# Which PSUM banks a decoder's token mixers take: single banks for columns and projections, pairs for spatial products, scores and turns

## The chip, the cores and the metric

The kernel runs on one core of a Trainium2 chip. The metric is the device time of one execution in microseconds (us). Times of single instructions come from a profile of one execution; they are counted from the start of its span.

## The reference

Two decoder layers over 256 positions of width 1024, in float32. Layer 0 mixes positions with a chunked gMLP (mixer A), layer 1 with block-sparse attention that at this length is plain causal attention over one block with a relative-position bias (mixer B, MoBA). After each mixer comes a gated MLP with a causal convolution of width 3, and after each of the four parts x <- LayerNorm(alpha x + f(x)).

```python
def chunked_gmlp(x, w_in, ln_g, ln_b, w_s, b_s, w_out):
    z = jax.nn.gelu(x @ w_in)
    u, v = jnp.split(z, 2, axis=-1)
    v = layer_norm(v, ln_g, ln_b)
    v = v.reshape(B, nc, GMLP_CHUNK, GMLP_GROUPS, GMLP_GROUP_DIM)
    w = jnp.where(causal[None], w_s, jnp.zeros_like(w_s))
    sv = jnp.einsum('gts,bnsgc->bntgc', w, v) + b_s.T[None, None, :, :, None]
    return (u * sv.reshape(B, S, GMLP_WIDTH)) @ w_out

def moba_attention(x, w_qkv, w_o, rel_bias):   # cut to what is left at S = 256
    q, k, v = ...                               # 16 heads of 64, q scaled
    s = q @ k.T + bias[rel_bucket(t - s)]       # -inf above the diagonal
    return softmax(s) @ v @ w_o

def conv_ffn(x, w_up, conv_w, conv_b, w_down):
    h = x @ w_up
    hc = conv_b + sum(conv_w[j] * shifted(h, j) for j in range(3))
    g, val = jnp.split(hc, 2, axis=-1)
    return (jax.nn.gelu(g) * val) @ w_down
```

## The kernel before

Every large product is made of float32 operands split in two parts, a high one (rounded by ScalarE, a Copy) and a low one (what is left, a subtraction on VectorE); three products high x high, high x low, low x high are added up in PSUM. Weights come by DMA in chunks of 1 MB into two buffers (raw) and are split into whi and wlo, of which ten half chunks are kept; the next chunk's loading is written down when the last product of an earlier one is (`spent`).

The program first writes down every operation in a plan, each with its engine, its cost and the buffers that it reads and writes. The planner (`Plan.emit`) then plays the plan through with these costs and gives each engine's instructions an order. On TensorE the bulk products keep the order in which they were written down; operations marked fill (spatial products, scores, turns, applies, transposes) go between them, as soon as the plan believes their inputs ready. Each engine then runs its order strictly, and waits where an input is late. `plan.later(ns, fn)` writes something down only after so many ns of TensorE's planned work.

PSUM has eight banks of 512 columns. Four are tiles of their own (`bank0` to `bank3` in the program, drawn as `bank`), four are the halves of two tiles of two banks each (`twos0`, `twos1`, the pairs; drawn as `twos`). The choice of a bank is made when an operation is written down:

```python
    def bank(long=False):
        free = [i for i in ALONE if not bank_of[i][2]]
        return taken(min(free, key=lambda i: bank_of[i][0]), long) if free else half(long)

    def couple(j):
        return j + BANKS // 2, j + BANKS // 2 + len(twos)

    def half(long=False):

        j = min((j for j in range(len(twos)) if not all(bank_of[i][2] for i in couple(j))),
                key=lambda j: max(bank_of[i][0] for i in couple(j)))
        return taken(min((i for i in couple(j) if not bank_of[i][2]), key=lambda i: bank_of[i][0]), long)
```

So `bank()` gives the single bank that was taken longest ago (a half, if all four are held for long), `half()` a half of the pair that was taken longest ago, `couple(j)` names the two halves of pair j, and `taken(i, long)` takes bank i and lets its new user wait for the one before. The plan follows banks; the program that is made from it guards tiles by its own means.

- Mixer A (`gmlp`): the v half of the input product goes by rows into the four single banks, held for long, until a GELU on ScalarE reads them; then v is normalized on VectorE. The u half goes by columns of 128: eight columns g, each of 24 products of 256 columns (`cols_times`) into a `half()`, and a GELU on ScalarE. The spatial product of group g (`spatial`, fill) also goes into a `half()`; VectorE adds the bias and multiplies by u. Five of them are written down between the columns, three during the output product (`project_out("a_out")`), whose four row pieces are single banks.
- MoBA (`moba`): the values go by rows into the halves of the two pairs (row block t = 0 into pair 0, t = 1 into pair 1), products over k = 0 to 4 for both row blocks first, then the rest, then the split. At that time the last two pieces of the down-projection before it (`project_out("f_dn0")`) and the transposes of its LayerNorm are still being read. For each pair of heads i then: q and k as columns (`project(i, 0)` and `project(i, 1)`, 24 products each into a `half()`, then a copy, a high and a low part), scores of the pair before (`scores`, two single banks, one for each head), the softmax on VectorE and ScalarE, turns (`turn`: three transposes of each head into a single bank, then the split), applies (`apply`, one bank). The last turns and applies are written down during the output product (`project_out("b_o")`), whose four row pieces are the four single banks.
- The up-projection (`conv_up`) uses both pairs in turn, two banks at a time.

In the rows below a line of the program can be that of a helper: L326 is a product (`mms`), L332 a transpose, L338 a ScalarE operation (`act`), L344 a VectorE operation of two tensors (`tt`), L348 one with a scalar, L351 the normalization, L825 to L834 the softmax. Tile names: xt is the transposed x, `ff` and `rr` are two large scratch buffers (q, k, u, softmax; h, v, applied heads), `qk` the parts of q and k.

Of the kernel before, what the change touches and what calls it, by code (L numbers as in the profile page):

```python
# [18 lines left out]
P = 128  # L19
# [6 lines left out]
NT = S // P  # L26
# [197 lines left out]
def trunk_kernel(ctx: ExitStack, tc: tile.TileContext, a: dict, out: bass.AP):  # L224
# [53 lines left out]
    def taken(i, long):  # L278
        old = bank_of[i][1]
        b = Buf(banks[i], [old] if old else [])  # L280
        state["age"] += 1
        bank_of[i] = (state["age"], b, long)
        return b
# [13 lines that stand above are left out]
# [342 lines left out]
    def gmlp():  # L639
        at = xt_at(xh, xl)  # L640
        pieces = [[(o, HALF, bank(True)) for o in (0, HALF)] for _ in range(NT)]
        order = [(k, t) for k in range(4) for t in range(NT)] + [(k, t) for t in range(NT) for k in range(4, KT)]
        v = []
        for k, t in order:
            rows_step(pieces[t], *at(k, t), *sub("a_v", k // 2, k % 2), k == 0, k == KT - 1)
            if t == NT - 1 and k % 2:
                spent("a_v", k // 2)
            if (k, t) == (3, NT - 1):
                rows = ln_rows(0)
                ws, bs = load_mixer()  # L650
            if k == KT - 1:
                vt = place("ff", HALF + t * D, D)
                for o, n, b in pieces[t]:
                    act(vt.ap[:, o:o + n], b.ap, AF.Gelu_apprx_tanh, [b], [(vt, range(o // S, (o + n) // S))],
                        psum=True, table="gelu")
                    done_with(b)
                st, mean, rstd = stats(vt, vt.ap, [(0, HALF), (HALF, HALF)])
                scaled(vt, vt.ap, st, mean, rstd, rows)
                v.append(vt)
        load_rest()  # L660
        mh, ml = place("rr", 0, KT * S), place("rr", KT * S, KT * S)
        hv, lv = (b.ap.rearrange("p (k s) -> p k s", k=KT) for b in (mh, ml))
        uring = Places("ff", [0, S, HALF + 2 * D, HALF + 2 * D + S], S)
        yring = Places("ff", range(5120, 6144, S), S)
        us = {}

        def spatial(g):
            b, y = half(), yring.new()
            mms([(b.ap[:, c * P:(c + 1) * P], v[c].ap[:, g * P:(g + 1) * P], ws[1][:, g, :], True, True)
                 for c in range(NT)], [(v[c], [g // 2]) for c in range(NT)] + [ws[0]], [b], fill=True)  # L670
            y3 = y.ap.rearrange("p (c t) -> p c t", c=NT)
            tt(y3, b.ap[:, :S].rearrange("p (c t) -> p c t", c=NT), bs[1][:, g:g + 1, :].to_broadcast([P, NT, P]),
               ALU.add, [b, bs[0]], [y])
            tt(y.ap, y.ap, us[g].ap, ALU.mult, [y, us[g]], [y])
            split((mh, [g], hv[:, g, :]), (ml, [g], lv[:, g, :]), (y, [0], y.ap))

        for g in range(GROUPS):
            b = half()
            cols_times(b, xh, xl, *sub("a_u", g // 2, g % 2))
            if g % 2:  # L680
                spent("a_u", g // 2)
            us[g] = uring.new()
            act(us[g].ap, b.ap[:, :S], AF.Gelu_apprx_tanh, [b], [us[g]], psum=True, table="gelu")
            if g >= 3:
                spatial(g - 3)
        for g in range(GROUPS - 3, GROUPS):
            plan.later(600 * (g - GROUPS + 4), lambda g=g: spatial(g))
        return lambda k, t: (hv[:, k, t * P:(t + 1) * P], lv[:, k, t * P:(t + 1) * P], [(mh, [k]), (ml, [k])])
# [69 lines left out]
    def moba(h, l, scr):  # L758
# [9 lines left out]
        ohv, olv = (b.ap.rearrange("p (k s) -> p k s", k=KT) for b in (oh, ol))  # L768
        vhv, vlv = (b.ap.rearrange("p (t d) -> p t d", t=NT) for b in (vh, vl))
        at = xt_at(h, l)  # L770
        pieces = [[(o, HALF, taken(i, True)) for o, i in zip((0, HALF), couple(j))] for j in range(NT)]
        for ks in (range(5), range(5, KT)):
            for t in range(NT):
                for k in ks:
# [10 lines left out]
        held, biases = {}, {}  # L785

        def project(i, j):
            b, t = half(), qkring[j].new()
            cols_times(b, h, l, *sub("b_qk", i, j))

            n, at2, scale = (P, P, DH ** -0.5) if j == 0 else (S, 0, 1.0)
            src, (th, tl) = b.ap[:, at2:at2 + n], (x.new() for x in qkparts[j])
            act(t.ap, b.ap[:, :P], AF.Copy, [b], [t], scale=scale, psum=True)
            act(th.ap, src, AF.Copy, [b], [th], scale=scale, psum=True)
            stt(tl.ap, src, scale, th.ap.bitcast(F32), ALU.mult, ALU.subtract, [b, th], [tl])
            t = (t, th, tl)
            held.setdefault(i, []).append(t)
            if j == 0:
                biases[i] = bring.new()
                load(biases[i].ap, bass.AP(tensor=scr.ap.tensor, offset=scr.ap.offset + 2 * i * DIST,  # L800
                                           ap=[[1, P], [DIST, 2], [1, S]]), [biases[i]], [scr])
            else:
                spent("b_qk", i)

        def scores(i):
            ((q0, qh, ql), (k0, kh, kl)), bias = held[i], biases[i]
            bank2 = [bank() for _ in range(2)]


            def both(o, seq):  # L810
                return [(bank2[hh].ap[:, o[0]:o[1]], x.ap[hh * DH:(hh + 1) * DH], y.ap[hh * DH:(hh + 1) * DH],
                         n == 0, n == len(seq) - 1) for n, (x, y) in enumerate(seq) for hh in range(2)]

            mms(both((0, P), [(q0, k0)]) + both((P, P + S), [(qh, kh), (qh, kl), (ql, kh)]),
                [q0, qh, ql, k0, kh, kl], bank2, fill=True)
            held[i] = [softmax(bank2[hh], bias, hh) for hh in range(2)]
# [20 lines left out]

        def turn(i):
            ph, pl = (x.new() for x in pring)
            for hh in range(2):  # L840
                e, b = held[i][hh], bank()

                transposes([(b.ap[:, c * P:(c + 1) * P], e.ap[:, c * P:(c + 1) * P]) for c in range(3)],
                           [(e, [0, 1])], [b])
                sl = slice(hh * (P + S), (hh + 1) * (P + S))
                split((ph, [hh], ph.ap[:, sl]), (pl, [hh], pl.ap[:, sl]), (b, [0], b.ap[:, :P + S]), psum=True)
            held[i] = ph, pl
# [124 lines left out]
```

## Time and profile before

| what | value |
|---|---|
| time, median of 3 runs | 578.51 us (577.9 to 579.87) |
| profiled execution: its own time | 579.16 us |
| profiled execution: span from first to last instruction | 577.5 us |
| mean granted TensorE clock, share of full speed | 0.997 |
| TensorE (PE) busy | 560.1 us, 97% of the span |
| VectorE (DVE) busy | 473.7 us, 82% |
| ScalarE (ACT) busy | 361.9 us, 63% |

A busy time is the sum over an engine's instructions, where they overlap counted once. The ends of products are modelled: 0.28 us for a product of 256 columns, though the next one starts earlier. A row of the order of time gives start, duration, engine, line, operation, output <- inputs, shapes and how many were merged; in brackets stands how long the engine was idle before it, and what ended that.

### The profile page before, as it was taken

The page shows a single profiled execution, that of the slowest core. Times are in us where ns is not written, and L with a number is a line of the kernel's source. Part 1 is how long each engine was busy: PE and PEld are TensorE (multiplying, and loading weights), DVE is VectorE, ACT ScalarE, POOL GpSimd, SP SyncE. Part 2 cuts the span into 40 slices and gives each one's busy share as a digit, 9 for nine tenths or more (in the row PEclk, how much of TensorE's full clock was granted, in tenths as well). Part 3 has the DMA queues.
Part 4 walks back from the last instruction along what each step waited for, and adds up shares of the span by engine and source line. Part 5 has one row for each costly group of instructions (what it writes and reads, how often), then busy time and mean ns, then how long its engine had stood idle before and what let it go on. Part 6 is the DMA issues. An engine that isn't in the chain of part 4 may idle for free.

```text
span 577.5 us, 8559 instructions
## 1 busy us (share of the span) xinstructions
PE 560.1 (97%) x3210; PEld 485.9 (84%) x3210; DVE 473.7 (82%) x885; ACT 361.9 (63%) x660; POOL 11.3 (2%) x17
## 2 busy tenths in 40 slices
PE   6998999999999999999999999999999999999994
PEld 4798888888888878888889998888888888888884
DVE  5587989999999997558878889879999999996426
ACT  5555567776677685435568777658777778785300
POOL 0020010000000000001000000000000000000001
PEclk9999999999999999999999999999999999999998
DMA  7887544537454567742663442515456555567202
GB/s 260 330 336 274 199 145 151 215 145 259 188 211 156 210 230 267 259 169 87 250 250 117 181 165 92 201 73 183 183 188 254 199 170 211 219 218 255 110 1 73
DMA packets 20133, 110.93 MB, mean 192 GB/s; under 512 B 2251, under 2 KB 6268, under 8 KB 7676
## 3 DMA queue, kind: packets, MB, share of 16 engines
q1 hardware_dynamic: 20092, 110.39, 53.0%
q8 instruction: 25, 0.41, 0.3%
q14 instruction: 16, 0.13, 0.1%
HBM read 109.31 MB, written 1.07 MB: 191 GB/s over the span
## 4 chain that ended last, share of the span: by engine, by line
PE 92%; DVE 3%; DMA 2%; ACT 2%; issue 0%; SPq 0%; DVEq 0%; ACTq 0%
PE twos L326 60%; PE bank L326 29%; DMA raw<-in_a_v 2%; PE bank L332 2%; DVE wlo L344 1%; DVE rr L344 1%; ACT ff L338 1%; DVE x L348 0%; ACT whi L338 0%; ACT rr L338 0%; SPq L355 0%; DVE ff L825 0%; PE twos L332 0%; DVE ff L834 0%; DVE stat L494 0%
## 5 line engine op out<-in xcount | busy, mean ns | idle before, releaser
L326 PE MATMUL twos<-xt,whi 128*128 128x512 f32 (+1 forms) x1024 | 295.1, 354 | 2.0 <-ACT ff L338 1.5
L344 DVE TENSOR_TENSOR wlo<-raw,whi 128x1024 fp32r<-128x1024 f32 (+1 forms) x212 | 228.4, 1098 | 30.8 <-ACT whi L338 30.3
L326 PE MATMUL twos<-xt,wlo 128*128 128x256 f32 x832 | 231.5, 278 | 0.0
L338 ACT ACTIVATE whi<-raw 128x1024 fp32r<-128x1024 f32 (+1 forms) x212 | 195.0, 954 | 56.7 <-DMA raw<-in_f_up 18.2
L326 PEld LDWEIGHTS twos<-xt,whi 128*128 128x128 f32 x1024 | 179.5, 189 | 31.7 <-ACT ff L338 2.4
L326 PEld LDWEIGHTS twos<-xt,wlo 128*128 128x128 f32 x832 | 156.8, 188 | 0.1
L326 PE MATMUL bank<-whi,rr 128*128 128x512 f32 x432 | 135.2, 391 | 0.4 <-DVE smax L825 0.4
L326 PEld LDWEIGHTS bank<-whi,rr 128*128 128x128 f32 x432 | 81.1, 188 | 18.0 <-issue 0.6
L326 PE MATMUL bank<-wlo,rr 128*128 128x512 f32 x216 | 84.1, 389 | 0.0
L348 DVE SCALAR_TENSOR_TENSOR ff<-ff,convc 128x255 f32<-128x255 f32 (+1 forms) x160 | 69.1, 477 | 0.0
L338 ACT ACTIVATE ff<-twos 128x512 f32<-128x512 f32 (+2 forms) x64 | 31.4, 491 | 53.4 <-PE twos L326 52.6
L326 PEld LDWEIGHTS bank<-wlo,rr 128*128 128x128 f32 x216 | 40.6, 188 | 8.1
L338 ACT ACTIVATE ff<-ff,convc 128x256 f32<-128x256 f32 x80 | 45.5, 592 | 2.9 <-DVE ff L344 2.5
L344 DVE TENSOR_TENSOR ff<-twos,ff 128x512 f32<-128x512 f32 (+1 forms) x48 | 30.9, 645 | 16.0 <-ACT ff L338 11.7
L326 PE MATMUL twos<-whi,xt 128*128 128x512 f32 x128 | 42.1, 396 | 0.5 <-DVE x L348 0.5
L338 ACT ACTIVATE ff<-bank,lncol 128x128 f32<-128x128 f32 x48 | 18.9, 460 | 29.1 <-PE bank L332 28.4
L348 DVE SCALAR_TENSOR_TENSOR x<-x,bank 128x512 f32<-128x512 f32 x16 | 11.0, 686 | 23.7 <-PE bank L326 23.6
L326 PEld LDWEIGHTS twos<-whi,xt 128*128 128x128 f32 x128 | 24.1, 188 | 5.7 <-DVE x L348 0.9
L326 PE MATMUL bank<-whi,xt 128*128 128x512 f32 x64 | 21.9, 420 | 5.1 <-DVE xt L361 5.0
L338 ACT ACTIVATE rr<-ff 128x256 fp32r<-128x256 f32 x52 | 21.0, 406 | 7.4 <-DVE ff L344 7.4
L326 PE MATMUL twos<-wlo,xt 128*128 128x512 f32 x64 | 25.0, 390 | 0.0
L344 DVE TENSOR_TENSOR ff<-ff 128x256 f32<-128x256 f32 x52 | 21.6, 418 | 0.5 <-ACT ff L338 0.2
(67 smaller groups left out, 416.9 us busy)
## 6 DMA issues: line engine op xcount, KB each, us to landing
raw<-in_f_up SPq DMA_DIRECT2D x44, 1024.0 KB, 4.8
raw<-in_f_dn SPq DMA_DIRECT2D x22, 1024.0 KB, 4.8
raw<-in_b_qk SPq DMA_DIRECT2D x8, 1024.0 KB, 4.8
lnrow<-in_lnrow SPq DMA_DIRECT2D x5, 1024.0 KB, 6.7
raw<-in_a_u SPq DMA_DIRECT2D x4, 1024.0 KB, 5.3
raw<-in_a_out SPq DMA_DIRECT2D x4, 1024.0 KB, 4.9
raw<-in_b_v SPq DMA_DIRECT2D x4, 1024.0 KB, 4.8
raw<-in_b_o SPq DMA_DIRECT2D x4, 1024.0 KB, 4.8
```

What stands on the lines that cost most here:

```text
L326: nc.tensor.matmul(o, l, x, start=start, stop=stop)
L332: nc.tensor.transpose(o, x, ident.ap)
L338: plan.op("act", ns, lambda: nc.scalar.activation(o, x, func, **kw), r, w, table=table)
L344: dve(70 + 1.04 * flat(x), lambda: nc.vector.tensor_tensor(o, x, y, op=op), r, w)
L348: lambda: nc.vector.scalar_tensor_tensor(o, x, s, y, op0=op0, op1=op1), r, w)
```

## The change

Columns of u and the projections of q and k take a single bank. Scores take both halves of pair 0, turns both halves of pair 1, and the turns of the two heads become one group of six transposes, written down ahead of both splits. The spatial products stay with `half()`; with the columns gone they are alone in the pairs. The value rows of MoBA take that pair first whose last taking lies further back. Nothing else is edited; the planner then makes a new order.

```diff
         for g in range(GROUPS):
-            b = half()
+            b = bank()
             cols_times(b, xh, xl, *sub("a_u", g // 2, g % 2))
...
-        pieces = [[(o, HALF, taken(i, True)) for o, i in zip((0, HALF), couple(j))] for j in range(NT)]
+        free_first = sorted(range(NT), key=lambda j: max(bank_of[i][0] for i in couple(j)))
+        pieces = [[(o, HALF, taken(i, True)) for o, i in zip((0, HALF), couple(j))] for j in free_first]
...
         def project(i, j):
-            b, t = half(), qkring[j].new()
+            b, t = bank(), qkring[j].new()
...
         def scores(i):
             ((q0, qh, ql), (k0, kh, kl)), bias = held[i], biases[i]
-            bank2 = [bank() for _ in range(2)]
+            bank2 = [taken(x, False) for x in couple(0)]
...
         def turn(i):
             ph, pl = (x.new() for x in pring)
-            for hh in range(2):
-                e, b = held[i][hh], bank()
-
-                transposes([(b.ap[:, c * P:(c + 1) * P], e.ap[:, c * P:(c + 1) * P]) for c in range(3)],
-                           [(e, [0, 1])], [b])
+            bs = [taken(x, False) for x in couple(1)]
+
+            transposes([(b.ap[:, c * P:(c + 1) * P], e.ap[:, c * P:(c + 1) * P])
+                        for e, b in zip(held[i], bs) for c in range(3)], [(e, [0, 1]) for e in held[i]], bs)
+            for hh, b in enumerate(bs):
                 sl = slice(hh * (P + S), (hh + 1) * (P + S))
                 split((ph, [hh], ph.ap[:, sl]), (pl, [hh], pl.ap[:, sl]), (b, [0], b.ap[:, :P + S]), psum=True)
             held[i] = ph, pl
```

## Rows read from the trace of the kernel before

**Rows 1.** The page's first part: busy time of each engine, its share of the span, its instructions.

```profile
PE 560.1 (97%) x3210; PEld 485.9 (84%) x3210; DVE 473.7 (82%) x885; ACT 361.9 (63%) x660; POOL 11.3 (2%) x17
```

**Rows 2.** Busy time of each engine in four stretches: Mixer A's columns, the up-projection of layer 0, the middle of MoBA, the end of MoBA. After the stretch and its length stand PE, PEld, DVE, ACT and POOL, then the granted clock, the DMA engines' share and GB/s.

```profile
31.00:60.00 29.00, 27.38 (x222) 26.51 (x222) 24.15 (x43) 15.73 (x26) 3.50 (x3) 1.00 0.80 297
97.00:207.00 110.00, 110.00 (x637) 96.20 (x636) 102.92 (x178) 81.00 (x138) 0.00 (x0) 1.00 0.55 200
301.00:350.00 49.00, 49.00 (x412) 46.61 (x412) 42.44 (x140) 37.82 (x108) 0.00 (x0) 1.00 0.44 154
350.00:369.00 19.00, 17.70 (x116) 14.97 (x115) 17.46 (x53) 13.85 (x37) 0.00 (x0) 1.00 0.50 167
```

**Rows 3.** Who TensorE's products waited for over the whole execution: us in total, times, the longest.

```profile
PE bank L326 <- DVE xt L361: 5.0, 1, 5.0
PE twos L326 <- ACT ff L338: 1.5, 3, 0.5
PE bank L326 <- DVE wlo L344: 0.8, 1, 0.8
PE bank L326 <- ACT ff L338: 0.6, 1, 0.6
PE twos L326 <- DVE x L348: 0.5, 1, 0.5
PE bank L326 <- DVE smax L825: 0.4, 1, 0.4
PE twos L326 <- DVE rr L344: 0.4, 1, 0.4
PE bank L326 <- DVE qk L348: 0.3, 1, 0.3
```

**Rows 4.** Order of time in Mixer A, 40 to 57 us: products of the columns (twos<-xt), of a spatial product (twos<-ff), then the GELU of columns 2 and 3 on ScalarE, and VectorE's addition to a spatial product.

```profile
43.56 0.28 PE L326 MATMUL twos<-xt,wlo 128*128 128x256 f32 x1
43.92 0.28 PE L326 MATMUL twos<-xt,wlo 128*128 128x256 f32 x1
44.68 0.50 PE L326 MATMUL twos<-xt,whi 128*128 128x256 f32 x2 [0.47 <-ACT ff L338]
...
48.77 0.28 PE L326 MATMUL twos<-xt,wlo 128*128 128x256 f32 x1
49.58 0.50 PE L326 MATMUL twos<-xt,whi 128*128 128x256 f32 x2 [0.53 <-ACT ff L338]
...
52.55 0.61 PE L326 MATMUL twos<-ff 128*128 128x128 f32 x4
53.25 0.50 PE L326 MATMUL twos<-xt,whi 128*128 128x256 f32 x2
...
55.74 0.28 PE L326 MATMUL twos<-xt,wlo 128*128 128x256 f32 x1
56.54 0.51 PE L326 MATMUL twos<-xt,whi 128*128 128x256 f32 x2 [0.52 <-ACT ff L338]
...
41.03 0.39 ACT L338 ACTIVATE ff<-twos 128x256 f32<-128x256 f32 x1 [0.56 <-DVE ff L344]
44.24 0.38 ACT L338 ACTIVATE ff<-twos 128x256 f32<-128x256 f32 x1 [2.83 <-PE twos L326]
...
40.57 0.42 DVE L344 TENSOR_TENSOR ff<-twos,ff 128x256 f32<-128x256 f32 x1 [0.73 <-PE twos L326]
```

**Rows 5.** Order of time where the values of MoBA begin: TensorE (the products of the values, twos<-whi,xt, and the transposes of the second row block's LayerNorm), then VectorE (the addition of the last piece of the down-projection, and the normalization).

```profile
270.44 0.50 PE L326 MATMUL twos<-whi,xt 128*128 128x512 f32 x1 [0.51 <-DVE x L348]
...
274.00 1.30 PE L332 MATMUL bank<-ident,x 128*128 128x128 f32 x8
...
269.96 0.42 DVE L348 SCALAR_TENSOR_TENSOR x<-x,twos 128x256 f32<-128x256 f32 x1
...
273.36 1.38 DVE L351 TENSOR_SCALAR x<-x,stat 128x256 f32<-128x256 f32 x4 [0.44 <-POOL stat L500]
```

**Rows 6.** Order of time between the first q and the first k of MoBA: TensorE's first product of k, and VectorE's last low part of the values.

```profile
296.28 0.50 PE L326 MATMUL twos<-xt,whi 128*128 128x256 f32 x2 [0.40 <-DVE rr L344]
...
295.53 0.69 DVE L344 TENSOR_TENSOR rr<-twos,rr 128x512 fp32r<-128x512 f32 x1 [0.67 <-ACT rr L338]
```

**Rows 7.** Order of time at the end of MoBA: TensorE (the turn of the last pair but one's second head; the last scores in two rows; the first product of the output projection; the product of its last k that needs the low part), then VectorE (the scaling of that second head's softmax; the low parts of the last apply).

```profile
356.89 0.55 PE L332 MATMUL bank<-ident,ff 128*128 128x128 f32 x3
358.01 0.49 PE L326 MATMUL bank<-ff 64*128 64x128 f32 x4 [0.57 <-ACT ff L338]
...
358.95 0.50 PE L326 MATMUL bank<-qk,qk 64*128 64x256 f32 x4 [0.33 <-DVE qk L348]
...
361.10 0.51 PE L326 MATMUL bank<-whi,rr 128*128 128x512 f32 x1 [0.40 <-DVE smax L825]
...
372.33 0.62 PE L326 MATMUL bank<-whi,rr 128*128 128x512 f32 x2
...
356.29 0.55 DVE L834 TENSOR_SCALAR ff<-ff,smax 128x256 f32<-128x256 f32 x2
...
370.13 0.86 DVE L344 TENSOR_TENSOR rr<-twos,rr 64x256 fp32r<-64x256 f32 x2 [0.38 <-ACT rr L338]
```

**Rows 8.** All groups of instructions by line and shape: the splits of a half chunk of weights on VectorE (count, busy us in all, mean ns of one, idle time of VectorE before them).

```profile
L344 DVE TENSOR_TENSOR wlo<-raw,whi 128x1024 fp32r<-128x1024 f32 x164 | 197.3, 1219 | 28.9 <-ACT whi L338 28.7
```

## The prediction

> **What bounds the kernel now.** I read the busy shares first, then the busy time by stage, then who TensorE waits for, and last the order of time around each of those waits. TensorE is busy 97% of the span and VectorE 82% [rows 1], so only a wait that ends on TensorE can be worth anything. By stage, the middle of MoBA (301 to 350 us) and the up-projection (97 to 207 us) show no TensorE idle time at all: 49.00 of 49 and 110.00 of 110 us [rows 2]. Whatever the change does to the order there, it can only lose. What is to be had lies in Mixer A's column stage (31 to 60 us: 27.38 of 29 us busy) and where MoBA ends (350 to 369 us: 17.70 of 19) [rows 2], and in two short waits between them [rows 3]. The clock is granted at its upper level (2.4 GHz, share 1.00) in all four stretches [rows 2], so it plays no part.
>
> One correction is needed to read these idle times. A 256-column product is drawn as 0.28 us, but three of them start within 0.36 us (43.56 to 43.92) [rows 4], so the next one is due 0.12 us after the last start and the real loss is the listed idle time plus about 0.16 us.
>
> **Mixer A: columns out of the pairs.** Column 3 ends at 43.84 us (43.56 + 0.28), yet its GELU on ScalarE starts only at 44.24, just after the next column's first three products have ended (43.92 + 0.28 = 44.20), and those products' successor starts at 44.68, after that GELU [rows 4]. By the allocation, column 3 and column 4 are in different banks of the same two-bank tile: half() takes turns between the pairs, and one spatial product between each two columns sends all columns from 3 on to the second pair. So an access to one half of a pair waits for accesses to the other half, in the order in which they are written out. The same shows without TensorE: the GELU of column 2 waits until 41.03 for VectorE's read of a spatial product (40.57, 0.42 us long) in the other half of the first pair [rows 4].
>
> The Trainium skill (PSUM — Partial Sum Buffer, section PSUM bank collisions raise a hardware error) has the rule to guard PSUM by bank and quadrant; by it two halves need no wait for each other, and this part would be worth 0, not the sum below. The trace disagrees here: 0.56 us of ScalarE's idle time at 41.03 falls on the other bank's reader [rows 4].
>
> The four losses are 44.68 - 43.92 - 0.12 = 0.64, 49.58 - 48.77 - 0.12 = 0.69, 53.25 - 52.55 - 4 x 0.11 = 0.26 (four passes of a spatial product, (0.61 - 0.28) / 3 = 0.11 each) and 56.54 - 55.74 - 0.12 = 0.68: 2.27 us [rows 4]. After the change columns rotate over four single banks, so a column meets its own bank's GELU four columns later (over 11 us, at 24 x 0.12 = 2.88 us each), and the spatial products take turns between the pairs. I take all 2.27. The bounds: 2.27 if nothing replaces the waits, 0 if the first rival holds. The output product then takes over the banks of columns 4 to 7; it meets the last one's GELU in its fourth group, nine 512-column products after its first, and a GELU is 0.38 us [rows 4]: no cost. What hides the shorter stage is weights that are split in time. VectorE has 29 - 24.15 = 4.9 us free in this stage and 7.1 in the up-projection [rows 2], against 2.3 us less time: enough.
>
> **MoBA's values: the pair free longest goes first.** Now the first row block takes the first pair, which the last piece of the down-projection still holds: its second group waits for VectorE's addition at 269.96, and loses 0.51 + 0.16 = 0.67 us [rows 5]. The other pair's piece was added earlier, so the wait goes. But the eight transposes at 274.00 are tied to VectorE's normalization at 273.36 to 274.74, which the change does not move [rows 5]. If they keep their place after the same 18 products, TensorE reaches them 0.67 us earlier and waits there instead: gain 0. If the planner, which knew the old wait, puts three more products ahead of them: 0.67. I take 0.4.
>
> **The first projections.** The first k waits for the split of the second row block's value halves: VectorE ends at 296.22 and TensorE starts at 296.28, 0.40 + 0.16 = 0.56 us late [rows 6]. In a single bank it has nothing to wait for: 0.56, or at least 0 if something else stops it there. The products behind it read rows and weights that were there before 296 us, or TensorE would have waited for them too [rows 3].
>
> **Middle of MoBA.** Products, transposes and splits keep their counts and sizes, and single banks are reused after four takers (three takers a pair of heads, where it was five). Against 0 us of idle time the gain is 0 [rows 2]. Six transposes in one group are the same six transposes (three take 0.55 us or less, [rows 7]). The first head's three now wait for the second head's softmax; the price is taken as 0, since the apply comes a whole iteration later. Its bad case is a rival below.
>
> **The end of MoBA.** TensorE waits three times: at 358.01 for ScalarE's copy of the last k (0.57), at 358.95 for its low part (0.33), and at 361.10 for VectorE's maximum over the last scores (0.40) [rows 7]. In each it has nothing else, since the output product's single banks are those of the last scores and turns. With 0.16 us each that is 1.78 us. Afterwards those four banks come from projections and applies that were read long before, so the output product can begin under all three waits. What ends last then is the last pair's chain: its low part is ready at 370.99 (370.13 + 0.86), and the product that needs it starts at 372.33 [rows 7], a slack of 1.3 us. The chain depends on the last scores, which can't start sooner. So TensorE may come 1.3 us earlier, and beyond that it waits for the chain: 1.3 us. Bounds: 0.56, if only the third wait goes (the scores stay in front), and 1.78, if the chain shortens too. The last two applies now go to the pair of the last scores, whose maximum still holds TensorE up at 361.10; the first of these is needed one step before the product at 372.33, some ten microseconds on [rows 7], so that costs nothing.
>
> **The sum.** 2.27 + 0.4 + 0.56 + 1.3 = 4.5 us. The profiled execution took 579.16 us, 0.65 more than the median of the runs, 578.51; taken from its own time the sum gives 574.6, and from the median 574.0, which is the forecast. Its own range is 573.2 (2.27 + 0.67 + 0.56 + 1.78 = 5.3 gained) to 575.8 (one wait of Mixer A stays, nothing at the values, 0.56 at the end: 1.6 + 0 + 0.56 + 0.56 = 2.7).
>
> **Rivals.** First, Mixer A's waits do not come from sharing a tile but from a GELU that is late anyway. Then 2.27 stays and 2.2 us are gained: 576.3. For it: only the order of time speaks of sharing. Against it: ScalarE was idle for 2.83 us before the GELU at 44.24 [rows 4], so it was not late by itself. This is also what the skill's PSUM rule would make of it. 8%.
>
> Second, the gain of Mixer A is handed back, since VectorE, busy 102.92 of 110 us in the up-projection [rows 2], splits weights too late for a TensorE that comes sooner. Again 576.3. Against it: TensorE does not wait for a split weight in that stage at all, and the free time adds up to 12 us. 8%.
>
> Third, no change. The spatial products lose the GELU that held their bank, so the planner puts them as soon as it believes the normalized v to be ready; if VectorE is behind by one weight split (1.22 us, [rows 8]) at four of them, 4.9 us go again and the time is 578.5 - 4.5 + 4.9 = 578.9. For it: VectorE is 83% busy there [rows 2]. Against it: no wait of TensorE for the normalized v is listed now [rows 3]. 10%.
>
> Fourth, slower. The group of six stands in TensorE's order behind the second head's scaling. In one case the margin is 0.05 us (356.29 + 0.55 = 356.84, transposes at 356.89) [rows 7]. If VectorE puts one weight split (1.22 us, [rows 8]) ahead of it in each of the eight pairs, TensorE waits 8 x 1.22 = 9.8 us, with projections queued behind it: 578.5 - 4.5 + 9.8 = 583.8. It decides from 4.5 / 8 = 0.57 us a pair. Against it: today's second group already stands behind the same scaling and no idle time came of it [rows 2]. 6%.
>
> **Chances.** The forecast's mechanism has 68%. Faster or slower by 0.3% is 1.7 us, about what a measurement of this kernel can tell: below 576.8 or above 580.2. Faster: 0.68 and most of the first two rivals (0.12) make 0.80. Same: their rest and the third, 0.13. Slower: 0.07. The range, 572.6 to 577.2, takes in both 576.3 cases and, below, the gain of 5.3 us with the scatter of the runs (0.6 below their median).
>
> **What would show it.** Right: between 31 and 60 us no GELU waits for a group of the next column, and the output product starts 2 us or more earlier; the first k starts right behind the first q; where MoBA ends, output products stand between the last projection and the last scores, and the next wait is for the last apply's low part. Wrong: transposes that wait for VectorE's scaling in the middle of MoBA, spatial products that wait for the normalized v, or waits for weights after 60 us.

## The result and the profile after

The changed kernel takes 574.21 us (median; 572.72 to 575.85) against 578.93 for the kernel before, measured beside it: a ratio of 0.9921, with a 95% interval of 0.9898 to 0.9944. The forecast was 574.0 us, with a range of 572.6 to 577.2 and a chance of 0.80 for faster.

The profiled execution of the changed kernel is its slowest: 575.85 us. First the busy times, then the four stretches of [rows 2] (length, then PE, PEld, DVE, ACT, POOL, the granted clock, the DMA share, GB/s), then who TensorE waited for (us, times, the longest).

```profile
PE 559.4 (97%) x3210; PEld 485.7 (85%) x3210; DVE 473.2 (82%) x885; ACT 359.6 (63%) x660; POOL 11.5 (2%) x17
```

```profile
31.00:60.00 29.00, 28.73 (x233) 28.07 (x232) 28.07 (x47) 17.22 (x28) 3.69 (x3) 1.00 0.81 300
97.00:207.00 110.00, 110.00 (x636) 96.15 (x634) 103.04 (x179) 81.14 (x138) 0.00 (x0) 1.00 0.55 197
301.00:350.00 49.00, 49.00 (x406) 46.14 (x406) 43.63 (x144) 39.51 (x110) 0.00 (x0) 1.00 0.51 178
350.00:369.00 19.00, 18.78 (x115) 15.58 (x114) 16.75 (x46) 12.70 (x38) 0.00 (x0) 1.00 0.30 113
```

```profile
PE bank L326 <- DVE xt L361: 5.0, 1, 5.0
PE bank L326 <- DVE wlo L344: 1.5, 2, 0.8
PE twos L326 <- DVE ff L348: 0.3, 1, 0.3
PE twos L326 <- DVE smax L826: 0.2, 1, 0.2
```

Of the waits in [rows 3] five groups are gone, those for ScalarE's ff (two) and for VectorE's x, rr and qk, the wait for smax fell from 0.4 to 0.2, one of 0.3 us for VectorE's ff (the normalized v) is new, and TensorE's busy time in Mixer A's columns rose from 27.38 to 28.73 of 29 us. The work is the same (3210 products); the holes between the products became smaller. The second wait for wlo is a weight split late by 0.76 us at 24.28 us, ahead of everything that the change touches.

Busy time can't say where the 4.7 us lie, since it counts overlapping products. The starts of TensorE's products can. These five of the kernel before mark the first column of Mixer A, the first LayerNorm transposes behind Mixer A, the first product of the values, the first q, and the first LayerNorm transposes behind MoBA:

```profile
31.29 0.40 PE L326 MATMUL twos<-xt,whi 128*128 128x256 f32 x2
...
78.22 1.03 PE L332 MATMUL bank<-ident,x 128*128 128x128 f32 x8
...
269.07 0.40 PE L326 MATMUL twos<-whi,xt 128*128 128x512 f32 x1
...
292.85 0.40 PE L326 MATMUL twos<-xt,whi 128*128 128x256 f32 x2
...
380.72 1.03 PE L332 MATMUL bank<-ident,x 128*128 128x128 f32 x8
```

The same five of the changed kernel:

```profile
32.33 0.40 PE L326 MATMUL bank<-xt,whi 128*128 128x256 f32 x2
...
77.40 1.03 PE L332 MATMUL bank<-ident,x 128*128 128x128 f32 x8
...
268.26 0.40 PE L326 MATMUL twos<-whi,xt 128*128 128x512 f32 x1
...
290.96 0.40 PE L326 MATMUL bank<-xt,whi 128*128 128x256 f32 x2
...
377.39 1.03 PE L332 MATMUL bank<-ident,x 128*128 128x128 f32 x8
```

Mixer A takes 45.07 instead of 46.93 us, the values 22.70 instead of 23.78, q to the end of MoBA 86.43 instead of 87.87. Between them nothing moved: from the transposes behind Mixer A to the values it is 190.86 us against 190.85. The three differences make 1.86 + 1.08 + 1.44 = 4.38 us, of which the later first column (32.33 for 31.29) takes 1.04 back in this execution.

The table gives the same three stretches for every kernel of the study, each from its own trace; e1 to e9 are the edited kernels of the next section, and after_again is the changed kernel once more. A trace is one execution, but these stretches repeat to some 0.05 us where no load is late and TensorE's order is the same, while the timings carry intervals of over a microsecond. One of e9's six executions, 698.04 us at a granted clock of 0.755 where the other five have 0.995 to 0.998, is left out of its row.

| kernel | Mixer A, us | values, us | q to end of MoBA, us | median, us | before beside it | ratio (95%) |
|---|---|---|---|---|---|---|
| before | 46.93 | 23.78 | 87.87 | | | |
| after | 45.07 | 22.70 | 86.43 | 574.21 | 578.93 | 0.9921 (0.9898 to 0.9944) |
| after_again | 44.28 | 22.70 | 86.40 | 574.45 | 579.23 | 0.9920 (0.9899 to 0.9940) |
| e1_columns_only | 44.28 | 23.78 | 87.83 | 575.94 | 578.99 | 0.9936 (0.9911 to 0.9962) |
| e2_all_but_columns | 46.92 | 22.71 | 86.44 | 576.12 | 578.99 | 0.9943 (0.9920 to 0.9966) |
| e3_spatials_single | 45.03 | 23.76 | 87.86 | 576.92 | 578.99 | 0.9954 (0.9935 to 0.9973) |
| e4_one_pair | 49.09 | 23.80 | 87.82 | 581.17 | 578.99 | 1.0034 (1.0016 to 1.0053) |
| e5_turns_two_groups | 44.29 | 22.74 | 87.40 | 575.22 | 579.42 | 0.9931 (0.9908 to 0.9955) |
| e6_fixed_pairs | 46.24 | 23.80 | 86.97 | 575.80 | 579.42 | 0.9942 (0.9922 to 0.9962) |
| e7_last_scores_single | 44.29 | 22.70 | 87.59 | 574.55 | 579.42 | 0.9924 (0.9895 to 0.9953) |
| e8_fills_later | 44.29 | 22.74 | 87.74 | 575.78 | 579.42 | 0.9937 (0.9913 to 0.9960) |
| e9_turns_single_applies_pair | 44.29 | 22.73 | 86.59 | 574.13 | 579.23 | 0.9912 (0.9890 to 0.9933) |

### The profile page after: what moved, and what is told of

Same layout as the page of the kernel before. It is cut to its first block, busy times and chain, and to the rows that moved or that the text cites. A ratio compares the mean times of both kernels' runs of the same rounds, so it can differ in the third digit from the quotient of the medians.

```text
span 574.1 us, 8566 instructions
## 1 busy us (share of the span) xinstructions
PE 559.4 (97%) x3210; PEld 485.7 (85%) x3210; DVE 473.2 (82%) x885; ACT 359.6 (63%) x660; POOL 11.5 (2%) x17
## 3 DMA queue, kind: packets, MB, share of 16 engines
HBM read 109.31 MB, written 1.07 MB: 192 GB/s over the span
## 4 chain that ended last, share of the span: by engine, by line
PE 91%; DMA 5%; DVE 2%; SPq 1%; ACT 1%; issue 1%; DVEq 0%; ACTq 0%
PE twos L326 51%; PE bank L326 37%; DMA raw<-in_a_v 3%; DMA raw<-in_a_u 2%; DVE wlo L344 1%; PE bank L332 1%; PE twos L332 1%; SPq L355 1%; ACT whi L338 0%; DVE x L348 0%; DVE ff L826 0%; ACT rr L338 0%; DVE rr L344 0%; DVE ff L348 0%; DVE stat L494 0%
## 5 line engine op out<-in xcount | busy, mean ns | idle before, releaser
L326 PE MATMUL twos<-xt,whi 128*128 128x512 f32 x640 | 222.2, 394 | 0.0
L326 PE MATMUL twos<-xt,wlo 128*128 128x256 f32 x640 | 177.3, 277 | 0.0
L326 PEld LDWEIGHTS twos<-xt,whi 128*128 128x128 f32 x640 | 120.0, 188 | 27.7
L326 PEld LDWEIGHTS twos<-xt,wlo 128*128 128x128 f32 x640 | 120.2, 188 | 0.1
L326 PE MATMUL bank<-xt,whi 128*128 128x256 f32 x384 | 71.2, 286 | 0.0
L348 DVE SCALAR_TENSOR_TENSOR ff<-ff,convc 128x254 f32<-128x254 f32 (+1 forms) x160 | 69.8, 478 | 0.1
L326 PEld LDWEIGHTS bank<-xt,whi 128*128 128x128 f32 x384 | 59.7, 191 | 0.8
L326 PE MATMUL bank<-xt,wlo 128*128 128x256 f32 x192 | 54.3, 283 | 0.0
L338 ACT ACTIVATE ff<-twos 128x512 f32<-128x512 f32 x40 | 23.8, 595 | 44.6 <-PE twos L326 44.3
L326 PEld LDWEIGHTS bank<-xt,wlo 128*128 128x128 f32 x192 | 36.7, 191 | 0.0
```

Source lines behind the costliest of these rows:

```text
L326: nc.tensor.matmul(o, l, x, start=start, stop=stop)
L338: plan.op("act", ns, lambda: nc.scalar.activation(o, x, func, **kw), r, w, table=table)
L348: lambda: nc.vector.scalar_tensor_tensor(o, x, s, y, op0=op0, op1=op1), r, w)
```

## The experiments

**One part alone, and all the others.** The first run makes only the column edit, in the kernel before; the second takes only that edit out of the changed kernel.

```diff
 # e1_columns_only, against before
-            b = half()
+            b = bank()
             cols_times(b, xh, xl, *sub("a_u", g // 2, g % 2))
```

> The kernel before with one edit: Mixer A's columns in single banks. Theory (a tile of two banks is guarded as a whole): the four waits of columns for the GELU before them go, 2.27 us, less the new waits for the normalized v that the changed kernel shows (41.60: 0.64 - 0.22 = 0.42; 46.13: 0.17): 1.7 to 2.3 us faster than the kernel before, with no GELU among the releasers of TensorE's products in Mixer A. The waits at MoBA's values, first k and end stay as they are. Rival (banks are guarded one by one, the GELU is late by itself): TensorE still waits for GELUs, no gain.

```diff
 # e2_all_but_columns, against after
-            b = bank()
+            b = half()
             cols_times(b, xh, xl, *sub("a_u", g // 2, g % 2))
```

> The changed kernel with its columns put back into halves of the pairs. Theory: the four waits of Mixer A are back (about 0.5 us idle each), the three places in MoBA stay mended; 2.2 to 3.0 us faster than the kernel before, by 1.08 at the values, 0.3 to 0.6 at the first projections and 1.2 to 1.5 at the end of MoBA as the two profiles show them. If the parts do not add up, the sum of this run's gain and that of the columns alone differs from the 4.7 us of the whole change by more than 1.3 us.

Measured: 575.94 and 576.12 us. The two traces split the gain cleanly. The columns alone shorten Mixer A by 2.65 us and leave the other two stretches where they were; the rest alone leaves Mixer A at 46.92 and brings 1.07 and 1.43. In e1 no product waits for a GELU between 26 and 80 us; in e2 the waits of [rows 3] for it are back (1.5 us, 3 times). By the medians the two parts gain 3.05 and 2.87, together more than the 4.7 of the whole; by the traces 2.65 + 2.50 = 5.15. Both lie within what the intervals leave open. For e1 the expectation was too low (1.7 to 2.3 us): the waits for the normalized v, which it took over from the changed kernel's first trace, are not there, and it left out the late second products that are counted below.

**What makes the columns wait.** The prediction's reading is that an access to one half of a pair waits for accesses to the other half. Two runs change only where things stand. In e3 the columns stay in halves, but the first four spatial products move to single banks, so the columns alternate between the pairs. In e4 all columns go to the two halves of one pair.

```diff
 # e3_spatials_single, against before
-            b, y = half(), yring.new()
+            b, y = bank() if g < 4 else half(), yring.new()
 # e4_one_pair, against before
-            b = half()
+            b = taken(couple(1)[g % 2], False)
             cols_times(b, xh, xl, *sub("a_u", g // 2, g % 2))
```

> The kernel before, with its columns left in halves of the pairs, but the first four spatial products in single banks. Without a spatial product between them the columns take turns between the two pairs, so no column meets the GELU of the column before it in its own tile. Theory (whole tile): the waits for GELUs go although every column still has a half of a pair: 1.7 to 2.3 us faster. Rival (what helps is a bank of its own, or more banks for columns): the columns keep four halves as before, no gain, and waits of about 0.5 us each for a GELU remain.

> The kernel before, with all eight columns in the two halves of the second pair, one after the other. Theory (whole tile): now seven columns, not four, meet the GELU of the column before; three more waits of 0.64 to 0.69 us: 1.9 to 2.1 us slower than the kernel before, with seven waits for GELUs on TensorE between 34 and 58 us. Rival (banks guarded one by one): a column's bank is read two columns (5.8 us) before it is taken again, no more waits than in the kernel before, same time.

Measured: 576.92 and 581.17 us. In e3 no column waits for a GELU, though all columns are still in pairs; Mixer A is 1.90 us shorter, with one new short wait for the normalized v (taken up with the last run):

```profile
40.41 0.94 PE L326 MATMUL bank<-ff 128*128 128x128 f32 x6 [0.20 <-DVE ff L348]
```

In e4 seven columns wait instead of four. Order of time on TensorE: the first column, the first and the last of the waiting ones, the transposes behind Mixer A.

```profile
30.84 0.40 PE L326 MATMUL twos<-xt,whi 128*128 128x256 f32 x2
...
34.71 0.50 PE L326 MATMUL twos<-xt,whi 128*128 128x256 f32 x2 [0.47 <-ACT ff L338]
...
58.26 0.50 PE L326 MATMUL twos<-xt,whi 128*128 128x256 f32 x2 [0.52 <-ACT ff L338]
...
79.93 1.03 PE L332 MATMUL bank<-ident,x 128*128 128x128 f32 x8
```

Who weight loads waited for in that kernel, 26 to 62 us:

```profile
PEld twos L326 <- ACT ff L338: 4.4, 7, 0.7
```

Mixer A is 2.16 us longer. Nothing was made slower in either run: only the neighbour in the tile was exchanged, and the waits went and came with it. So the waits follow the two-bank tile, and the first rival (the GELU is late anyway) falls. One more rival would fit e3 alone: there the columns rotate over four halves, where from column 3 on the kernel before had two. It does not fit e4, where two halves serve as before, and each column from the second on waits for the GELU of the column just ahead of it, which reads the other half. The Trainium skill (PSUM — Partial Sum Buffer, section PSUM bank collisions raise a hardware error) guards by bank and quadrant, by which neither run should have changed anything; the waits in this program differ from that, by -1.90 and +2.16 us. The guard is the program's own; no run here tells whether the chip would need it.

**The order of the pairs at the values.** In the changed kernel the values go back to the fixed order of pairs.

```diff
 # e6_fixed_pairs, against after
-        pieces = [... for j in free_first]
+        pieces = [... for j in range(NT)]
```

> The changed kernel with MoBA's first value rows always in the first pair, as before. Theory: the wait for the last addition of the down-projection is back (0.5 us idle, about 0.8 us lost with the restart), and with it the transposes that then meet VectorE: from the first product of the values to the first q 23.8 us as in the kernel before, not 22.7; 1.1 us slower than the changed kernel, 3.6 us faster than the kernel before. Rival (the order by free time brings nothing, the gain there came from elsewhere in the new order): 22.7 us, no difference.

Measured: 575.80 us, and the values take exactly the 23.80 us of before. The wait is the one of [rows 5], 0.51 us for VectorE's addition. The two rows before it are Mixer A of the same execution, ScalarE's high part of a weight chunk and a spatial product:

```profile
40.74 2.01 ACT L338 ACTIVATE whi<-raw 128x1024 fp32r<-128x1024 f32 x2 [1.98 <-DMA raw<-in_a_u]
...
41.31 0.94 PE L326 MATMUL twos<-ff 128*128 128x128 f32 x6 [1.04 <-DVE ff L348]
...
269.34 0.50 PE L326 MATMUL twos<-whi,xt 128*128 128x512 f32 x1 [0.51 <-DVE x L348]
```

So that edit is worth 1.1 us by itself. Two other things lengthen this kernel's trace. Mixer A's 46.24 us is not of the edit, which comes 200 us later: a load of weights came 1.98 us late. And q to the end of MoBA takes 0.54 us more than in the changed kernel, in another order of the planner: of the six applies up to the last projection five take 1.29 us or more, where it is three in the changed kernel. What else is in the 0.54 stays open. That 575.80 lies 3.6 us below the kernel before, as expected, therefore shows less than the 23.80 us do.

**The group of six.** The turn is undone into one group for each head, in the same pair.

```diff
 # e5_turns_two_groups, against after
-            transposes([... for e, b in zip(held[i], bs) for c in range(3)], [(e, [0, 1]) for e in held[i]], bs)
-            for hh, b in enumerate(bs):
+            for hh, (e, b) in enumerate(zip(held[i], bs)):
+                transposes([... for c in range(3)], [(e, [0, 1])], [b])
```

> The changed kernel with the turns back in two groups of three, in the two halves of the same pair. Theory (whole tile): the second head's transposes write a tile whose other half is being read for the first head's split, so TensorE waits for that split where it is written ahead of them: 1 to 6 us slower than the changed kernel, with transposes among TensorE's waits for VectorE or ScalarE. Rival (banks guarded one by one): no such wait; the first head's split starts earlier, and the short waits inside the applies of the changed kernel (0.1 to 0.4 us each at 309, 334, 343 and 349 us) go: 0.3 to 1 us faster than the changed kernel.

Measured: 575.22 us; q to the end of MoBA takes 0.97 us more than in the changed kernel, just under the 1 to 6 us expected. The same guard shows again: the second head's transposes wait for VectorE's split of the first head, in the other half.

```profile
304.67 0.55 PE L332 MATMUL twos<-ident,ff 128*128 128x128 f32 x3 [0.40 <-DVE rr L344]
```

Beside these 0.40 us the weight loads of such transposes wait at 329.04 and 362.08, 0.25 and 0.37 us, for ScalarE's high part. How the 0.97 us divide among these and the applies, four of which take 1.32 us, is not shown. One group for both heads goes with the move into a pair, then: written in two groups, the pair costs waits that the single banks of before didn't have.

**The end of MoBA.** The last scores and the last turn but one go back to single banks, which are then no longer free for the output projection.

```diff
 # e7_last_scores_single, against after
-            bank2 = [taken(x, False) for x in couple(0)]
+            bank2 = [taken(x, False) for x in couple(0)] if i < PAIRS - 1 else [bank() for _ in range(2)]
...
-            bs = [taken(x, False) for x in couple(1)]
+            bs = [taken(x, False) for x in couple(1)] if i != PAIRS - 2 else [bank() for _ in range(2)]
```

> The changed kernel with only the scores of the last pair of heads and the turns of the last but one back in single banks, so that the output projection takes those banks over as in the kernel before. Theory (the gain at the end comes from the output projection's banks being free): it starts again only after the maximum over the last scores; from the last projection's last product to the next LayerNorm's transposes 23.6 us and more, not 22.5; 1.1 us slower than the changed kernel. Rival (the gain there comes from the shorter queues of VectorE or from the six transposes): no difference.

Measured: 574.55 us by the runs, which can't be told from the changed kernel; by the trace the stretch takes 87.59 us, 1.16 more, and two waits of [rows 7] are back, for ScalarE's copy of the last k and for the maximum over the last scores:

```profile
352.42 0.49 PE L326 MATMUL bank<-ff 64*128 64x128 f32 x4 [0.99 <-ACT ff L338]
...
354.93 0.50 PE L326 MATMUL bank<-whi,rr 128*128 128x512 f32 x1 [0.44 <-DVE smax L826]
```

The four single banks that the output projection finds free are what the end gains by.

**Two tries at more.** In e8 the planner counts on 0.25 us more ahead of each fill. In e9 the turns keep the groups and single banks of before and the applies take a pair instead.

```diff
 # e8_fills_later, against after
-        return self.LATE[d.eng] + (150.0 if o.eng == "pe" else 0.0)
+        return self.LATE[d.eng] + (400.0 if o.fill else 150.0 if o.eng == "pe" else 0.0)
```

> The changed kernel with one number of its planner raised: the operations that TensorE fills in are taken to have their inputs 0.25 us later than now. If the short waits that are left on TensorE (inside the applies, before the spatial products, before the last applies: some 2 us in all in the changed kernel's trace) come from filling in too early, 0.5 to 1.5 us faster than the changed kernel. If the plan only moves them, within 0.5 us of it.

Measured: 575.78 us, the stretch 87.74, 1.31 more than after. The expectation was wrong: the later fills also put off the last pair's chain, and the output projection waits 0.86 us at its end for the high part of the last apply.

```profile
367.88 0.50 PE L326 MATMUL bank<-whi,rr 128*128 128x512 f32 x1 [0.86 <-ACT rr L338]
```

```diff
 # e9_turns_single_applies_pair, against after: turn() as in before, and
-            b = bank()
+            b = taken(couple(1)[i % 2], False)
             o3 = b.ap.rearrange("p (a b) -> p a b", a=2)
```

> The changed kernel with turns and applies exchanged: the turns of each head as a group of three in a single bank of its own, as in the kernel before, and the applies in the halves of the second pair. Theory: the short waits inside the applies in the middle of MoBA (0.13 to 0.36 us each, 1.1 us in all) come from the group of six, which delays the first head's split; with groups of three in tiles of their own they go, nothing shares a pair with a reader that is late, and the last applies no longer wait for the maximum over the last scores: from the first q to the LayerNorm after MoBA 85.0 to 86.0 us, where the changed kernel takes 86.4 and the kernel before 87.9; 0.5 to 1.4 us faster than the changed kernel. Rival (the applies wait for VectorE's queue, whatever the groups): 86.4 us or more, no gain over the changed kernel.

Measured: 574.13 us, the stretch 86.59: no gain on the changed kernel. The theory's 85.0 to 86.0 us failed, and the rival's number came (86.4 or more); that the applies wait for VectorE's queue, as the rival had it, is not what the one listed wait shows. The last apply but one stands close behind its turn, and waits for the turn's high part, which ScalarE ends at 356.43 (355.94 + 0.49):

```profile
356.48 1.67 PE L326 MATMUL twos<-rr 128*128 128x512 f32 x6 [0.58 <-ACT rr L338]
...
355.94 0.49 ACT L338 ACTIVATE rr<-bank 128x384 fp32r<-128x384 f32 x1 [1.21 <-PE bank L332]
```

**The changed kernel once more.** Its first profile had a late start and a short new wait in Mixer A; a second profile tells whether that belongs to the change.

> The changed kernel once more, unedited, beside the next one and the kernel before. Theory: 4.0 to 5.0 us faster than the kernel before; if the waits for the normalized v in Mixer A (0.42 and 0.18 us at 41.60 and 46.13 in its first trace) came from weights that were loaded late in that one execution, they are absent where the column stage begins without a second wait for weights at about 24 us, and from the first column to the next LayerNorm's transposes 44.3 us pass instead of 45.07. Rival: those waits are part of the changed order and come back.

Measured: 574.45 against 579.23 us, and Mixer A takes 44.28 us with no wait for the normalized v. TensorE's first column and the transposes behind Mixer A, then the last high part of a_u for which ScalarE waited:

```profile
30.16 0.40 PE L326 MATMUL bank<-xt,whi 128*128 128x256 f32 x2
...
74.44 1.03 PE L332 MATMUL bank<-ident,x 128*128 128x128 f32 x8
...
37.06 2.01 ACT L338 ACTIVATE whi<-raw 128x1024 fp32r<-128x1024 f32 x2 [0.28 <-DMA raw<-in_a_u]
```

In the first profile the same kernel had this (TensorE's spatial products, VectorE's scaling of v, ScalarE's high part of the weights):

```profile
40.96 0.39 PE L326 MATMUL twos<-ff 128*128 128x128 f32 x2
41.60 0.94 PE L326 MATMUL twos<-ff 128*128 128x128 f32 x6 [0.25 <-DVE ff L348]
...
41.06 0.48 DVE L348 SCALAR_TENSOR_TENSOR ff<-ff,stat,lnrow 128x256 f32<-128x256 f32 x1
...
41.08 2.01 ACT L338 ACTIVATE whi<-raw 128x1024 fp32r<-128x1024 f32 x2 [1.34 <-DMA raw<-in_a_u]
```

ScalarE waits 1.34 us for the load, and the third pass of the spatial products starts at 41.60, right behind the scaling (41.06 + 0.48 = 41.54). The wait of ScalarE for this last chunk and the length of Mixer A go together over nine traces in which no column waits for a GELU: 0.28 us or less in six of them, with 44.28 or 44.29; 1.29 us in e3, with 45.03; 1.34 here, with 45.07; 1.98 in e6, with 46.24. That the late load is the cause is read from these; no run delayed a load on purpose. Without this 0.79 us and the first column's 1.04, the first profile's 575.85 would be 574.0, near the median.

## Why the prediction was right, point by point

**What bounds it: right.** The gain came from waits that ended on TensorE, in the stages named, and the up-projection and the rest stayed where they were.

**Mixer A, 2.27 us: the mechanism right, the term too small.** It is 2.65 us where no load is late. The four waits of [rows 4] cost the listed idle time plus 0.16, as read; but the product behind each of them is late too. The row at 44.68 holds two products in 0.50 us, so the second starts at 44.90 (44.68 + 0.50 - 0.28), 0.22 us behind the first instead of 0.12. That is 0.10 us at each of four waits, 0.4 in all, and 2.27 + 0.4 = 2.67.

**The values, 0.4 us: the choice too low.** It is 1.08, above even the upper bound of 0.67. The planner did put three products more ahead of the transposes (21 instead of 18), which the prediction had left half open, and it also split them, with three more products between:

```profile
272.82 0.39 PE L326 MATMUL twos<-whi,xt 128*128 128x512 f32 x1
273.05 0.38 PE L332 MATMUL bank<-ident,x 128*128 128x128 f32 x2
273.18 0.48 PE L326 MATMUL twos<-whi,xt 128*128 128x512 f32 x1
273.96 0.82 PE L332 MATMUL bank<-ident,x 128*128 128x128 f32 x6
```

The eight transposes took 1.30 us at 274.00 [rows 5], since the normalization behind which they ran had not ended; eight that wait for nothing take 1.03 (77.40 above). Now two run early, and six behind it in 0.82. The bound held the wait (0.67, with its late second product 0.77) and left out this stall, some 0.27.

**The first projections, 0.56 us, and the middle, 0: one right, one wrong.** The first k starts right behind the first q:

```profile
293.72 0.28 PE L326 MATMUL bank<-xt,wlo 128*128 128x256 f32 x1
293.84 0.40 PE L326 MATMUL bank<-xt,whi 128*128 128x256 f32 x2
```

Its wait is gone (0.56, with the late second product 0.67). Yet from the first q to the last projection product the changed kernel needs 63.97 us for what took 63.93 with three transposes, or 0.33 us, less in it. Net it gained 0.29; 0.38 were lost in the middle. TensorE's applies show where: the six of before up to the last projection product take 1.21 or 1.22 us each, and of the changed kernel's six three take more, one 1.29 us (348.60) and the two shown here. Behind them stand a weight load of the second, and VectorE's low part of a q.

```profile
334.25 1.33 PE L326 MATMUL bank<-rr 128*128 128x512 f32 x6
342.95 1.32 PE L326 MATMUL bank<-rr 128*128 128x512 f32 x6
...
342.95 0.30 PEld L326 LDWEIGHTS bank<-rr 128*128 128x128 f32 x2 [0.20 <-DVE qk L348]
...
342.61 0.28 DVE L348 SCALAR_TENSOR_TENSOR qk<-bank,qk 128x128 fp32r<-128x128 f32 x1
```

The apply at 342.95 starts 0.15 us late, as VectorE's low part of the q just projected ends (342.61 + 0.28 = 342.89). With the 0.28 us by which the three are longer that is 0.43, about what was lost. So "it can only lose", the prediction's own sentence on this stretch, was right, and the 0 in its sum was too high: it weighed a loss only for the six transposes. Why the applies became longer stays open: by the allocation the bank of the apply at 342.95 was that of the q before, which had long been read, and in e9, where the applies don't use single banks, two of them still take 1.33 us.

**The end of MoBA, 1.3 us: right, at 1.15.** From the last projection product to the transposes it is 22.46 us, where before it was 23.94 with 0.33 us of transposes more in it. The last projection product of the kernel before:

```profile
356.78 0.28 PE L326 MATMUL twos<-xt,wlo 128*128 128x256 f32 x1
```

The end of the changed kernel, TensorE (first its last projection product), then VectorE's low part of the last apply:

```profile
354.93 0.28 PE L326 MATMUL bank<-xt,wlo 128*128 128x256 f32 x1
355.05 0.40 PE L326 MATMUL bank<-whi,rr 128*128 128x512 f32 x1
356.53 0.49 PE L326 MATMUL twos<-ff 64*128 64x128 f32 x4
357.34 0.50 PE L326 MATMUL bank<-whi,rr 128*128 128x512 f32 x1
359.22 1.31 PE L326 MATMUL twos<-rr 128*128 128x512 f32 x6 [0.22 <-DVE smax L826]
...
368.87 0.73 PE L326 MATMUL bank<-whi,rr 128*128 128x512 f32 x2
...
367.95 0.86 DVE L344 TENSOR_TENSOR rr<-twos,rr 64x256 fp32r<-64x256 f32 x2 [0.17 <-ACT rr L338]
```

Output products stand between the last projection and the last scores, as forecast, and where the chain ends, a product waits for the low part (367.95 + 0.86 = 368.81, product at 368.87), as forecast. One sentence was wrong: the first of the last applies, in the pair of the last scores, was to cost nothing. It comes at 359.22, not some ten microseconds later, and waits for the maximum over those scores, about 0.5 us with its late second product. It is a step that the planner takes as soon as it may, not when its result is needed.

**The rivals.** The first fell (e3, e4), the second too: the up-projection takes what it took. The third, that spatial products wait for the normalized v, is real but small: 0.79 us in the first execution, none in the second, instead of the 4.9 that would have undone the gain. The fourth, transposes that wait for the second head, didn't come: no such wait is listed, and undoing the group of six cost 0.97 us.

**The sum.** 4.5 was forecast, 2.65 + 1.08 + 0.29 + 1.15 = 5.2 is what the undisturbed stretches give, and 4.7 is what the runs give, whose intervals are over a microsecond to either side. Two terms were too small by 1.1 together and two too large by 0.4. So that 574.0 lies 0.2 us from the measured median is in part luck: the errors of the terms offset each other in part, the runs gain some 0.4 us less than the stretches add up to, and the kernel before took 578.93 us beside the changed one, 0.4 more than the 578.51 that the forecast started from.

**The signs.** That no GELU holds up a column, that the first k follows the first q, and that output products stand ahead of the last scores came as said. The output product of Mixer A starts 27.36 us behind the first column in the first profile, where it was 28.75 before, and 26.57 in the second: "2 us or more earlier" holds for the second alone (2.18; 1.39 in the first). The next wait at the end is for the maximum over the last scores, ahead of the one for the low part. Of the signs of being wrong, spatial products that wait for the normalized v came, in the first profile.

## What to carry to other kernels

A wait for a neighbour's reader shows as idle time that ends with an access to a buffer the waiting instruction doesn't use; look in the order of time for what shares its tile, and move the neighbour to test it. Neighbours that are written and read together (both heads' scores, both heads' transposes in one group) may share a tile; those that follow each other closely cost waits here (e4, e5). And a wait costs more than its listed idle time: read the starts of the products around it, the one behind it included, and ask of each step that a planner may move how early it can come, not how late it is needed.

## What the runs showed of the hardware that was not expected

The second product behind a wait of TensorE starts late as well: 0.22 us behind the first instead of 0.12 with 256 columns (44.68 and 44.90), 0.33 instead of 0.23 with 512 columns (359.22 and 359.55, then 359.78). The listed idle time of a wait of 0.47 us therefore stood for some 0.74 us of lost time.

The times of whole executions hid what the traces showed: e7 lost 1.16 us in its stretch, and its median is 0.3 us from that of the changed kernel, with an interval over a microsecond wide on either side.
